# Gathering the RG-LRU gate products of a hybrid decoder layer into four runs on TensorE

## The chip, the cores and the metric

The kernel runs on one core of one Trainium2 chip. The metric is device time in microseconds: the median over runs. Each core has the engines TensorE (PE in the profile), VectorE (DVE), ScalarE (ACT), GpSimd (POOL) and SyncE (SP, which issues most DMAs).

## The reference

One decoder layer on 1024 tokens of width 1024, with 16 meta tokens ahead of them. Cut to what matters here:

```python
u = rmsnorm(h, g_pre_mix)
q, k, v, xr, yr = split(u @ w_in)           # 512, 128, 128, 512, 512 columns
attn = sliding_window_attention_with_sinks(q, k, v, sinks)     # window 128
xr = causal_depthwise_conv(xr, conv_w, conv_b)                 # width 4
# RG-LRU: 8 blocks of 64 channels
r = sigmoid(einsum(xr, w_a) + b_a)          # the gates: a 64x64 product a block
i = sigmoid(einsum(xr, w_x) + b_x)
a = exp(-8 * r * softplus(-lam))
hr = scan(a, sqrt(1 - a*a) * i * xr)        # h[t] = a[t] h[t-1] + u[t]
rec = gelu(yr) * hr
h = h + rmsnorm(concat(attn, rec) @ w_out)
h = h + rmsnorm(relu(rmsnorm(h) @ w_ff1)**2 @ w_ff2)
```

## The kernel before

Every float32 operand of a matmul is split into a rounded high part and a low part (`split`, L94: a cast, mostly on ACT, then a subtraction on DVE), and a product is the sum of three matmuls, high by high, high by low and low by high (`mm3`, L123). Activations lie with channels on the 128 partitions and tokens along the row, in two pieces of 512 columns (`REAL2`) or three of at most 348 (`THIRDS`).

The input projection of a chunk of 128 channels against all tokens is `project` (L265): for each piece a bank of PSUM under the tag `acc` (two buffers), 24 matmuls into it, then a `sink` that copies the bank out. For the y columns there are four chunks, y0 to y3, each 2 x 24 matmuls; their sink is a DVE copy (L752). In the profile these matmuls appear as L125, L130 and L131 with `ps_acc<-a,ws`.

Attention goes in eight steps of two pairs of heads and a quarter of the tokens: `scores` (products, exponentials on ACT) and `attend` (transposes, POOL selects at L684, six value products a half into a bank `o` at L697, then the bank's two halves summed: an ACT copy at L706 and a DVE addition at L707, twice a step). While attention runs, one further projection is put in a step (`next_fill`, with a priority `FILL_LAG` = 1000 steps back); the last two of these eight are y0 and y1. Then come the gates.

`gates(c)` handles channel chunk c of four: it splits the conv's output, and for each third of the tokens it takes two banks (tags `s`, `pt`, `o` in turn, two buffers each) and issues six matmuls of 64 rows (L819). `s` picks the upper or the lower 64 partitions, so two neighbours with `s` = 0 and 1 use the two row halves of the array. That makes 18 products a chunk, 72 in all. ACT empties each bank with a sigmoid (`lut`, L82). `gather(c)` then exchanges halves between the two gates (DVE at L833, L835 and L836, POOL at L834), and `decay`, `recur` and `rec_out` go on to the recurrence; every function on ACT's tables is kept in program order by `lut`. Projections y2 and y3 and the output projection's products follow.

The order of instructions on each engine is found when the program is built, by a list scheduler with priorities (program order, unless deferred) over a simulated timeline; tiles of a tag wait for a free buffer. `behind(name, ins)` adds an ordering edge for that scheduler and no signal on the chip. `split`, `mm3`, `gates` and `project` are helpers, so one line of the profile may stand for many uses.

Of the kernel before, what the change touches and what calls it, by code (L numbers as in the profile page):

```python
# [9 lines left out]
F32 = mybir.dt.float32  # L10
F32R = mybir.dt.float32r
AF = mybir.ActivationFunctionType
ALU = mybir.AluOpType
# [3 lines left out]
P = 128  # L17
D = 1024
KC = D // P
T = 1024  # L20
NMETA = 16
# [3 lines left out]
NLRU = 4  # L25
# [12 lines left out]
def hybrid_layer(  # L38
# [6 lines left out]
    nc = tc.nc  # L45
# [4 lines left out]
    small = ctx.enter_context(tc.tile_pool(name="small", bufs=4))  # L50
# [4 lines left out]
    bufs = {"raw": 2, "ws": 5, "a": 16, "b": 17, "c": 8, "d": 4, "e": 2}  # L55
    uid = [0]

    def slot(tag, shape, dt=F32):
        uid[0] += 1
        return slab.tile(shape, dt, tag=tag, name=f"{tag}{uid[0]}", bufs=bufs[tag])  # L60

    def pair(tag, shape):
        return slot(tag, shape, F32R), slot(tag, shape, F32R)

    def bank(tag, shape=(P, 512)):
        uid[0] += 1
        return ps.tile(list(shape), F32, tag=tag, name=f"ps_{tag}{uid[0]}")

    def f32(ap):
        return ap.bitcast(F32)  # L70
# [10 lines left out]
    def lut(*args, **kwargs):  # L81
        ins = nc.scalar.activation(*args, **kwargs).ins  # L82
        if last_lut[0] is not None:
            tc.add_manual_dep(
                ins, last_lut[0],
                mybir.DependencyInfo(
                    mybir.DependencyClass.NoSync, mybir.DependencyReason.DATA
                ),
                reason="lut",
            )  # L90
        last_lut[0] = ins.name
        return ins

    def split(hi, lo, src, eng=None):  # L94
        if eng is None:
            nc.scalar.copy(hi, src)  # L96
        else:
            eng.tensor_copy(hi, src)
        low = nc.vector.tensor_tensor(lo, src, f32(hi), op=ALU.subtract).ins  # L99
        mark[0] = low.name  # L100
        return low
# [4 lines left out]
    def behind(name, *inss):  # L106
        for ins in inss:
            tc.add_manual_dep(
                ins, name,
                mybir.DependencyInfo(  # L110
                    mybir.DependencyClass.NoSync, mybir.DependencyReason.DATA
                ),
                reason="order",
            )
# [8 lines left out]
    def mm3(dst, lhs, rhs, start, stop, after=None):  # L123
        (lh, ll), (rh, rl) = lhs, rhs
        ins = nc.tensor.matmul(  # L125
            dst, lh, rh, start=start, stop=False, skip_group_check=True
        ).ins
        if after:
            behind(after, ins)
        nc.tensor.matmul(dst, lh, rl, start=False, stop=False, skip_group_check=True)  # L130
        last_mm[0] = nc.tensor.matmul(  # L131
            dst, ll, rh, start=False, stop=stop, skip_group_check=True
        ).ins.name
# [50 lines left out]
    eps_col = const.tile([P, 1], F32, name="eps_col")  # L184
# [44 lines left out]
    u = [pair("a", [P, TT]) for _ in range(KC)]  # L229
# [32 lines left out]
            chained(1, ins)  # L262
        return xn

    def project(w, pieces, sink):  # L265
        wh, wl = w
        for t0, n in pieces:
            acc = bank("acc")
            for kc in range(KC):
                uh, ul = u[kc]  # L270
                mm3(
                    acc[:, :n], (wh[:, kc, :], wl[:, kc, :]),
                    (uh[:, t0 : t0 + n], ul[:, t0 : t0 + n]),
                    kc == 0, kc == KC - 1,
                )
            sink(acc[:, :n], t0, n)

# [11 lines left out]
    REAL2 = [(16, 512), (528, 512)]  # L289
# [209 lines left out]
    for b in range(4):  # L499
# [3 lines left out]
        if b == 0:  # L503

            acc = [bank("acc"), bank("acc")]
# [11 lines left out]
            for w, (t0, n), sink, tag in (  # L517
                (wq, (16, 256), sink_q0, "o"), (wq1, (16, 256), sink_q1, "acc"),
            ):
                acc = bank(tag)  # L520
# [10 lines left out]
    for h in range(2):  # L531
        r, o, m = HALF[h], HALF[1 - h], slice(P - NMETA, 2 * P)
# [77 lines left out]
    def scores(jp, quarter):  # L610
# [57 lines left out]
            )  # L668
        return sn

    def attend(jp, quarter, sn):
        flat = sn.rearrange("p a b c -> p (a b c)")
        pp = []
        for h in range(2):

            ph, pl = (slot("c", [P, 4, 2, P], F32R) for _ in range(2))
            pt = bank("pt")
            for i in range(4):
                nc.tensor.transpose(pt[:, i * P : (i + 1) * P], sn[:, h, i, 0:P], ident)
            pt = pt.rearrange("p (a b) -> p a b", a=4)  # L680
            split(ph[:, :, 0], pl[:, :, 0], pt)
            for p_ in (ph, pl):
                for s, g, op in ((1, 1, ALU.is_ge), (0, -1, ALU.is_gt)):
                    nc.gpsimd.affine_select(  # L684
                        out=p_[:, :, s], in_=f32(p_[:, :, 0]), pattern=[[0, 4], [g, P]],
                        compare_op=op, fill=0.0, base=0, channel_multiplier=-g,
                    )
            pp.append((ph, pl))
        kb0 = 2 * quarter
        for h in range(2):  # L690
            po = bank("o")
            two = po.rearrange("p (j c) -> p j c", j=2)
            for n, (oc, pc, w) in enumerate(((0, 0, P), (0, P, 2 * P), (P, 3 * P, P))):
                kb = kb0 + n
                v = vk[h][:, kb - 1, :] if kb else vm[:, h, :]
                for k, p_ in enumerate(pp[h]):
                    nc.tensor.matmul(  # L697
                        two[:, :, oc : oc + w], v,
                        p_.rearrange("p (j i) s c -> p j (i s c)", j=2)[:, :, pc : pc + w],
                        start=n == 0 and k == 0, stop=n == 2 and k == 1,  # L700
                        skip_group_check=True,
                    )

            r, o = HALF[h], HALF[1 - h]
            whole = flat[r, 0:512]
            nc.scalar.copy(whole, po[o, :])  # L706
            nc.vector.tensor_tensor(whole, po[r, :], whole, op=ALU.add)  # L707
        ah, al = at[quarter // 2][jp]
        c = slice(256 * (quarter % 2), 256 * (quarter % 2) + 256)
        split(  # L710
            ah[:, :, c], al[:, :, c],
            flat[:, 0:512].rearrange("p (j c) -> p j c", j=2),
        )
# [4 lines left out]
    def conv(c, xr, tag="d"):  # L718
# [9 lines left out]
            )  # L728
        xc[c] = y

    ys, y_copies = [None] * NLRU, {}

    def fill_q(j):
# [13 lines left out]
    def fill_y(c):  # L747
        def run(w):
            y = slot("b" if c in (1, 2) else "d", [P, T])

            def sink(acc, t0, n):
                ins = nc.vector.tensor_copy(y[:, t0 - NMETA : t0 - NMETA + n], acc).ins  # L752
                y_copies.setdefault(c, ins.name)

            project(w, REAL2, sink)
            ys[c] = y
        return run

    qs = [q0, q1, None, None]
    fills = []  # L760
# [7 lines left out]
    loaded = [fills[0][0]()]  # L768

    def next_fill():  # L770
        i = len(loaded) - 1
        if i + 1 < len(fills):
            loaded.append(fills[i + 1][0]())
        else:
            loaded.append(None)
        fills[i][1](loaded[i])

    prev = None
    for jp in range(2):
        at_pair(jp)  # L780
        for quarter in range(4):
# [4 lines left out]
            if prev is not None:  # L786
                attend(*prev)
            prev = (jp, quarter, sn)
    attend(*prev)


# [10 lines left out]
    nc.vector.tensor_tensor(gw[:, 1], graw, f32(gw[:, 0]), op=ALU.subtract)  # L802

    rg = [None] * NLRU

    def gates(c):
        ch, cl = pair("b", [P, TT])
        split(ch, cl, xc[c])


        z = [slot("c", [P, TT]) for _ in range(2)]
        for t0, n in THIRDS:
            acc = []
            for s in range(2):
                flip[0] += 1
                acc.append(bank(("s", "pt", "o")[flip[0] % 3]))
            for k, (a, b) in enumerate(((0, ch), (0, cl), (1, ch))):
                for s in range(2):
                    nc.tensor.matmul(  # L819
                        acc[s][:, :n], gw[HALF[s], a, c, :], b[HALF[s], t0 : t0 + n],  # L820
                        start=k == 0, stop=k == 2, skip_group_check=True,
                    )
            for s in range(2):
                lut(
                    z[s][:, t0 : t0 + n], acc[s][:, :n], AF.Sigmoid,
                    bias=prm[:, c, 5 + s : 6 + s],
                )
        rg[c] = z


    def gather(c):
        z, gi = rg[c], slot("b" if c > 1 else "c", [P, TT])
        first = nc.vector.tensor_copy(gi[HALF[0]], z[0][HALF[1]]).ins  # L833
        nc.gpsimd.tensor_copy(z[0][HALF[1]], z[1][HALF[1]])  # L834
        nc.vector.tensor_copy(gi[HALF[1]], z[1][HALF[0]])  # L835
        nc.vector.tensor_tensor(gi, gi, xc[c], op=ALU.mult)  # L836
        rg[c] = z[0], gi
        return first
# [38 lines left out]
        wo[kc] = pair(tag, [P, D])  # L877
        split(wo[kc][0], wo[kc][1], wo_raw[kc], eng)

    for c in range(NLRU):  # L880
        gates(c)
        if c < 2:
            gather(c)
    next_fill()
    for c in (2, 3):
        behind(y_copies[2], gather(c))
    next_fill()
# [275 lines left out]
    for t in range(8):  # L1163
        po = pos[t] if t < 4 else out_banks(t)
# [191 lines left out]
    for n, p in enumerate(third):  # L1356
# [10 lines left out]
        if p not in a12_early:  # L1367
            y2 = bank(("acc", "s")[p % 2])
# [192 lines left out]
```

## Time and profile before

| | |
|---|---|
| median of 3 runs | 949.5 us (949.23 to 949.68) |
| the profiled execution | 949.03 us, span 947.3 us |
| TensorE | 937.9 us busy, 4584 matmuls |
| VectorE | 664.4 us busy |
| ScalarE | 505.0 us busy |
| GpSimd | 135.9 us busy |
| DMA | 134.91 MB, mean 142 GB/s |
| granted TensorE clock | 0.998 |

In the profile's lines, PE is TensorE's matmul, PEld its weight load, and `out<-in` names the written and the read tiles. In a timeline, the columns are the start, the duration, the engine, the line and the tiles; in brackets stands the engine's idle time before the instruction and what ended it. Matmuls are pipelined and their durations overlap, so the distance from start to start is the measure of what one costs.

### The profile page before, as it was taken

What the parts mean: (1) busy time and instruction counts of PE and PEld (TensorE: products, weight loads), DVE (VectorE), ACT (ScalarE), POOL (GpSimd) and SP (SyncE); (2) the same over time, 40 slices, a digit from 0 to 9 for tenths busy, and PEclk for the clock granted to TensorE, in tenths of its full rate; (3) what the DMA queues carried; (4) which work ended last, traced back from release to release, by engine and by line L of the source; (5) the groups of instructions that cost most, each with busy time, mean ns of one, the idle gap of its engine ahead of it and who ended that gap; (6) DMA issues with size and microseconds to landing.
All of it is one profiled execution on the core that took longest, in us unless ns stands there. A gap on an engine that the chain in (4) does not pass through costs nothing.

```text
span 947.3 us, 12174 instructions
## 1 busy us (share of the span) xinstructions
PE 937.9 (99%) x4584; PEld 784.8 (83%) x4584; DVE 664.4 (70%) x849; ACT 505.0 (53%) x844; POOL 135.9 (14%) x205
## 2 busy tenths in 40 slices
PE   9999999999999999999999999999999999999996
PEld 8999999878888878888888888888888888888885
DVE  6667788779977987665544465476667676779783
ACT  8546765569634664443655575654533443445441
POOL 4104437431021100010000000001111000001201
PEclk9999999999999999999999999999999999999999
DMA  8220011104259658574422363334777655537934
GB/s 273 57 68 23 24 45 45 45 23 141 82 194 273 200 180 283 188 258 134 156 89 89 111 215 120 109 111 114 198 170 178 206 179 192 194 126 209 238 64 89
DMA packets 97366, 134.91 MB, mean 142 GB/s; under 512 B 22230, under 2 KB 61158, under 8 KB 97308
## 3 DMA queue, kind: packets, MB, share of 16 engines
q1 hardware_dynamic: 87996, 108.64, 35.3%
q0 software_dynamic: 8880, 24.19, 11.9%
q10 hardware_dynamic: 432, 1.31, 0.4%
q8 instruction: 36, 0.59, 0.3%
q14 instruction: 22, 0.18, 0.1%
HBM read 112.55 MB, written 20.97 MB: 141 GB/s over the span
## 4 chain that ended last, share of the span: by engine, by line
PE 97%; DVE 1%; DMA 0%; ACT 0%; issue 0%; SPq 0%; DVEq 0%
PE ps_acc L125 12%; PE ps_acc L131 12%; PE ps_acc L130 12%; PE ps_pt L131 6%; PE ps_s L131 6%; PE ps_pt L125 6%; PE ps_pt L130 6%; PE ps_s L125 6%; PE ps_s L130 6%; PE ps_o L125 5%; PE ps_o L131 5%; PE ps_o L130 5%; PE ps_o L697 2%; PE ps_acc L282 1%; PE ps_s L629 1%; PE ps_s L633 1%
## 5 line engine op out<-in xcount | busy, mean ns | idle before, releaser
L99 DVE TENSOR_TENSOR ws<-raw,ws 128x1024 fp32r<-128x1024 f32 (+1 forms) x69 | 82.3, 1193 | 72.4 <-PE ps_o L130 23.1
L96 ACT CAST ws<-raw 128x1024 fp32r<-128x1024 f32 (+1 forms) x68 | 69.8, 1027 | 82.0 <-PE ps_o L130 33.6
L96 ACT CAST ws<-e 128x1024 fp32r<-128x1024 f32 x41 | 43.0, 1050 | 85.8 <-PE ps_o L130 38.2
L130 PE MATMUL ps_acc<-a,ws 128*128 128x512 f32 (+3 forms) x240 | 82.9, 346 | 0.0
L125 PE MATMUL ps_acc<-a,ws 128*128 128x512 f32 (+3 forms) x240 | 82.8, 346 | 0.0
L131 PE MATMUL ps_acc<-a,ws 128*128 128x512 f32 (+3 forms) x240 | 82.2, 343 | 0.0
L99 DVE TENSOR_TENSOR b<-b,b 128x1024 fp32r<-128x1024 f32 (+2 forms) x50 | 59.0, 1179 | 27.9 <-PE ps_o L130 22.6
L99 DVE TENSOR_TENSOR ws<-e,ws 128x1024 fp32r<-128x1024 f32 x41 | 50.2, 1223 | 31.7 <-ACT ws L96 18.4
L96 ACT CAST b<-b 128x1024 fp32r<-128x1024 f32 (+2 forms) x49 | 50.0, 1020 | 41.8 <-DVE b L1029 35.5
L684 POOL TENSOR_SCALAR_AFFINE_SELECT c<-c 128x512 fp32r<-128x512 f32 x64 | 55.0, 873 | 73.7 <-ACT c L96 64.2
L125 PEld LDWEIGHTS ps_acc<-a,ws 128*128 128x128 f32 x240 | 45.2, 189 | 4.3 <-issue 0.7
L131 PEld LDWEIGHTS ps_acc<-a,ws 128*128 128x128 f32 x240 | 45.2, 188 | 3.7 <-issue 0.2
L130 PEld LDWEIGHTS ps_acc<-a,ws 128*128 128x128 f32 x240 | 45.2, 188 | 3.6 <-issue 0.4
L131 PE MATMUL ps_acc<-ws,b 128*128 128x512 f32 (+1 forms) x120 | 46.3, 386 | 0.0
L130 PE MATMUL ps_acc<-ws,b 128*128 128x512 f32 (+1 forms) x120 | 46.2, 385 | 0.0
L125 PE MATMUL ps_acc<-ws,b 128*128 128x512 f32 (+1 forms) x120 | 46.0, 385 | 0.0
L125 PE MATMUL ps_pt<-ws,b 128*128 128x512 f32 x112 | 44.3, 395 | 0.0
L131 PE MATMUL ps_pt<-ws,b 128*128 128x512 f32 x112 | 44.2, 395 | 0.0
L130 PE MATMUL ps_pt<-ws,b 128*128 128x512 f32 x112 | 44.1, 394 | 0.0
L131 PE MATMUL ps_s<-ws,b 128*128 128x512 f32 x110 | 43.4, 394 | 0.0
L130 PE MATMUL ps_s<-ws,b 128*128 128x512 f32 x110 | 43.4, 394 | 0.0
L125 PE MATMUL ps_s<-ws,b 128*128 128x512 f32 x110 | 43.3, 394 | 0.0
(417 smaller groups left out, 2660.0 us busy)
## 6 DMA issues: line engine op xcount, KB each, us to landing
raw<-in_w_ff_dram SPq DMA_DIRECT2D x59, 512.0 KB, 3.9
e<-in_w_ff_dram SPq DMA_DIRECT2D x43, 512.0 KB, 3.5
a<-in_w_ff_dram SPq DMA_DIRECT2D x12, 512.0 KB, 6.0
s_dram<-a POOLq DMA_DIRECT2D x12, 512.0 KB, 4.1
raw<-in_w_in_dram SPq DMA_DIRECT2D x9, 512.0 KB, 3.6
c<-in_x_dram SPq DMA_DIRECT2D x8, 512.0 KB, 4.5
d<-in_x_dram SPq DMA_DIRECT2D x8, 512.0 KB, 3.4
out_dram<-raw SPq DMA_DIRECT2D x8, 512.0 KB
```

The lines of the kernel that those rows point to most:

```text
L96: nc.scalar.copy(hi, src)
L99: low = nc.vector.tensor_tensor(lo, src, f32(hi), op=ALU.subtract).ins
L125: ins = nc.tensor.matmul(dst, lh, rh, start=start, stop=False, skip_group_check=True).ins
L130: nc.tensor.matmul(dst, lh, rl, start=False, stop=False, skip_group_check=True)
L131: last_mm[0] = nc.tensor.matmul(dst, ll, rh, start=False, stop=stop, skip_group_check=True).ins.name
L282: last_mm[0] = nc.tensor.matmul(acc[:, :n], w[k // 2][:, kc, :], u[kc][k % 2][:, t0 : t0 + n], start=k == 0 and kc == 0, stop=k == last an ...
L629: nc.tensor.matmul(dst, q[h][:, c], hi, start=True, stop=False, skip_group_check=True,)
L633: nc.tensor.matmul(dst, q[h][:, c], lo, start=False, stop=True, skip_group_check=True,)
L684: nc.gpsimd.affine_select(out=p_[:, :, s], in_=f32(p_[:, :, 0]), pattern=[[0, 4], [g, P]], compare_op=op, fill=0.0, base=0, channel_multip ...
L697: nc.tensor.matmul(two[:, :, oc : oc + w], v, p_.rearrange("p (j i) s c -> p j (i s c)", j=2)[:, :, pc : pc + w], start=n == 0 and k == 0, ...
```

## The change

The gate products of a chunk are chained one behind the other, so that each chunk's 18 products stand together on PE. The first chunk's run is ordered behind the last DVE addition that reads a bank of value products (`drained`). y2 is no longer projected by `next_fill` but by `y2_products`: its first 24 products after the first chunk's gates in program order, not held; then five behind gates(0) and ahead of gates(1), five between gates(1) and gates(2), five between gates(2) and gates(3), and the last nine behind gates(3). y3's projection is held behind the last gate product, and its weights are loaded ahead of the gates. A sigmoid of one column stands in ACT's table order ahead of the first gate sigmoid.

```diff
--- before.py
+++ after.py
@@ -262,7 +262,7 @@
             chained(1, ins)
         return xn
 
-    def project(w, pieces, sink):
+    def project(w, pieces, sink, after=None):
         wh, wl = w
         for t0, n in pieces:
             acc = bank("acc")
@@ -271,7 +271,7 @@
                 mm3(
                     acc[:, :n], (wh[:, kc, :], wl[:, kc, :]),
                     (uh[:, t0 : t0 + n], ul[:, t0 : t0 + n]),
-                    kc == 0, kc == KC - 1,
+                    kc == 0, kc == KC - 1, after if kc == 0 else None,
                 )
             sink(acc[:, :n], t0, n)
 
@@ -668,6 +668,8 @@
             )
         return sn
 
+    drained = [None]
+
     def attend(jp, quarter, sn):
         flat = sn.rearrange("p a b c -> p (a b c)")
         pp = []
@@ -704,7 +706,9 @@
             r, o = HALF[h], HALF[1 - h]
             whole = flat[r, 0:512]
             nc.scalar.copy(whole, po[o, :])
-            nc.vector.tensor_tensor(whole, po[r, :], whole, op=ALU.add)
+            drained[0] = nc.vector.tensor_tensor(
+                whole, po[r, :], whole, op=ALU.add
+            ).ins.name
         ah, al = at[quarter // 2][jp]
         c = slice(256 * (quarter % 2), 256 * (quarter % 2) + 256)
         split(
@@ -728,6 +732,7 @@
             )
         xc[c] = y
 
+    gate_end = [None]
     ys, y_copies = [None] * NLRU, {}
 
     def fill_q(j):
@@ -752,7 +757,7 @@
                 ins = nc.vector.tensor_copy(y[:, t0 - NMETA : t0 - NMETA + n], acc).ins
                 y_copies.setdefault(c, ins.name)
 
-            project(w, REAL2, sink)
+            project(w, REAL2, sink, gate_end[0])
             ys[c] = y
         return run
 
@@ -802,10 +807,13 @@
     nc.vector.tensor_tensor(gw[:, 1], graw, f32(gw[:, 0]), op=ALU.subtract)
 
     rg = [None] * NLRU
+    warm = small.tile([P, 1], F32, name="warm", tag="warm", bufs=1)
+    lut(warm, eps_col, AF.Sigmoid)
 
     def gates(c):
         ch, cl = pair("b", [P, TT])
         split(ch, cl, xc[c])
+        start = last_mm3[0] if c else drained[0]
 
 
         z = [slot("c", [P, TT]) for _ in range(2)]
@@ -816,16 +824,22 @@
                 acc.append(bank(("s", "pt", "o")[flip[0] % 3]))
             for k, (a, b) in enumerate(((0, ch), (0, cl), (1, ch))):
                 for s in range(2):
-                    nc.tensor.matmul(
+                    ins = nc.tensor.matmul(
                         acc[s][:, :n], gw[HALF[s], a, c, :], b[HALF[s], t0 : t0 + n],
                         start=k == 0, stop=k == 2, skip_group_check=True,
-                    )
+                    ).ins
+                    if start:
+                        behind(start, ins)
+                    start = ins.name
+            gate_end[0] = start
             for s in range(2):
                 lut(
                     z[s][:, t0 : t0 + n], acc[s][:, :n], AF.Sigmoid,
                     bias=prm[:, c, 5 + s : 6 + s],
                 )
         rg[c] = z
+
+    last_mm3 = [None]
 
 
     def gather(c):
@@ -877,11 +891,45 @@
         wo[kc] = pair(tag, [P, D])
         split(wo[kc][0], wo[kc][1], wo_raw[kc], eng)
 
-    for c in range(NLRU):
+    loaded.append(fills[9][0]())
+    y2 = slot("b", [P, T])
+    wh, wl = loaded[8]
+    done_mm = 0
+
+    def y2_products(count):
+        nonlocal done_mm
+        for m in range(done_mm, done_mm + count):
+            half, kc, k = m // 24, m % 24 // 3, m % 3
+            t0, n = REAL2[half]
+            if m % 24 == 0:
+                y2_bank.append(bank("acc"))
+            uh, ul = u[kc]
+            ins = nc.tensor.matmul(
+                y2_bank[half], (wh, wh, wl)[k][:, kc, :],
+                (uh, ul, uh)[k][:, t0 : t0 + n],
+                start=m % 24 == 0, stop=m % 24 == 23, skip_group_check=True,
+            ).ins
+            if m == done_mm and m >= 24:
+                behind(gate_end[0], ins)
+            last_mm3[0] = ins.name
+            if m % 24 == 23:
+                copied = nc.vector.tensor_copy(
+                    y2[:, t0 - NMETA : t0 - NMETA + n], y2_bank[half]
+                ).ins
+                y_copies.setdefault(2, copied.name)
+        done_mm += count
+
+    y2_bank = []
+    gates(0)
+    gather(0)
+    y2_products(24)
+    for c in range(1, NLRU):
+        y2_products(5)
         gates(c)
         if c < 2:
             gather(c)
-    next_fill()
+    y2_products(48 - done_mm)
+    ys[2] = y2
     for c in (2, 3):
         behind(y_copies[2], gather(c))
     next_fill()
```

## The prediction

> **What bounds the kernel now.** I read the page first, then the PE groups and PE's timeline where the gate products stand, then the timelines of ACT, DVE and POOL over the same stretch, and last the place where PE next waits. The page:
>
> ```profile
> span 947.3 us, 12174 instructions
> ...
> PE 97%; DVE 1%; DMA 0%; ACT 0%; issue 0%; SPq 0%; DVEq 0%
> ```
>
> The chain that ended last is TensorE work nearly everywhere, so an edit is worth what it takes off PE's stream, less what PE then has to wait. The gate products lie among the y products. The groups of PE between two y products, the starts at 193.17 and 213.08 us:
>
> ```profile
> L819 PE MATMUL ps_s<-b,e 64*128 64x348 f32 x24 | 5.6, 341 | 0.0
> L819 PE MATMUL ps_pt<-b,e 64*128 64x348 f32 (+1 forms) x24 | 5.6, 349 | 0.0
> L130 PE MATMUL ps_acc<-a,ws 128*128 128x512 f32 x13 | 5.3, 410 | 0.0
> L819 PE MATMUL ps_o<-b,e 64*128 64x348 f32 (+1 forms) x24 | 5.2, 335 | 0.0
> L125 PE MATMUL ps_acc<-a,ws 128*128 128x512 f32 x12 | 5.1, 429 | 0.0
> L131 PE MATMUL ps_acc<-a,ws 128*128 128x512 f32 x13 | 5.1, 393 | 0.0
> L697 PE MATMUL ps_o<-c,b 128*128 128x256 f32 (+1 forms) x6 | 1.5, 354 | 0.0
> ```
>
> So this stretch of 213.08 - 193.17 = 19.91 us holds all 72 gate products (3 x 24), six value products (L697), and 12 + 13 + 13 y products with the last one's start as its end, that is 37 whole y intervals. Busy times overlap here, so I go by starts. PE's timeline (start, duration):
>
> ```profile
> 190.50 0.97 PE L697 MATMUL ps_o<-c,b 128*128 128x256 f32 x5
> 191.31 0.40 PE L130 MATMUL ps_acc<-a,ws 128*128 128x512 f32 x1
> ...
> 193.17 0.39 PE L125 MATMUL ps_acc<-a,ws 128*128 128x512 f32 x1
> ...
> 206.38 0.39 PE L131 MATMUL ps_acc<-a,ws 128*128 128x512 f32 x1
> 206.70 0.43 PE L819 MATMUL ps_pt<-b,e 64*128 64x348 f32 x1
> ...
> 206.97 0.32 PE L819 MATMUL ps_pt<-b,e 64*128 64x348 f32 x1
> ...
> 208.08 0.32 PE L819 MATMUL ps_s<-b,e 64*128 64x348 f32 x1
> ...
> 208.33 0.50 PE L125 MATMUL ps_acc<-a,ws 128*128 128x512 f32 x1
> 208.67 0.40 PE L130 MATMUL ps_acc<-a,ws 128*128 128x512 f32 x1
> ...
> 213.08 0.50 PE L131 MATMUL ps_acc<-a,ws 128*128 128x512 f32 x1
> ...
> 224.23 0.40 PE L131 MATMUL ps_acc<-a,ws 128*128 128x512 f32 x1
> ```
>
> The run from 206.70 to 208.08 is one of nine pairs, each pair on the two row halves side by side. It gives the prices. From the second pair to the ninth: (208.08 - 206.97) / 7 = 0.159 us a pair. From 213.08 to 224.23 lie 48 y intervals, the first behind a run; (11.15 - 0.11) / 48 = 0.230 us a y product. Around the run, four steps are longer than these: 206.38 to 206.70 is 0.32 (0.09 over), the first pair takes 0.27 (0.11 over), the last pair 0.25 (0.09 over), and 208.33 to 208.67 is 0.34 (0.11 over). Going into the half-height products and out again costs 0.40 us a run.
>
> **What the 72 products cost now, and in four runs.** Five value products take 191.31 - 190.50 = 0.81 us; the sixth I estimate at a fifth of that, 0.16. The stretch less its other work is 19.91 - 37 x 0.230 - 0.97 = 10.43 us for the gates. In four whole runs they cost 4 x (9 x 0.159 + 0.40) = 7.32 us. **PE's stream loses 3.1 us.** The rest of the 10.43 is crossings, and products that ran with no partner.
>
> **The hold and the one-column sigmoid.** ACT and POOL, with the idle time before and what ended it in brackets:
>
> ```profile
> 196.01 1.28 ACT L82 ACT_TABLE_LOAD   x1 [3.86 <-PE ps_s L819]
> 197.31 0.55 ACT L82 ACTIVATE c<-ps_s,prm 128x348 f32<-128x348 f32 x1
> 197.88 0.58 ACT L706 COPY c<-ps_o 64x512 f32<-64x512 f32 x1
> 198.48 1.06 ACT L96 CAST b<-b 128x1040 fp32r<-128x1040 f32 x1
> ...
> 199.89 0.61 ACT L96 CAST b<-c 128x512 fp32r<-128x512 f32 x1
> 200.40 0.55 ACT L82 ACTIVATE c<-ps_o,prm 128x348 f32<-128x348 f32 x1
> 200.85 0.55 ACT L82 ACTIVATE c<-ps_s,prm 128x348 f32<-128x348 f32 x1
> ...
> 214.02 0.56 ACT L82 ACTIVATE c<-ps_o,prm 128x344 f32<-128x344 f32 x1
> ```
>
> ```profile
> 189.29 4.82 POOL L684 TENSOR_SCALAR_AFFINE_SELECT c<-c 128x512 fp32r<-128x512 f32 x3 [0.36 <-DVE c L99]
> ```
>
> Today the first gate sigmoid and its table load stand on ACT ahead of the copy at L706, and that copy's DVE partner (L707) is the read behind which the change holds the first gate product. With the gates held, ACT has nothing ahead of L706. POOL's selects end at 189.29 + 4.82 = 194.1; the five value products end some 0.9 us later; L706 (0.58) and L707 (0.69) with hand-overs bring the read's end to about 197.0. On PE meanwhile: of y2's first 24 products 14 are left at 193.17 (38 to the end of both halves, less 24), so without gates they reach 193.17 + 14 x 0.230 + 0.97 = 197.4. The hold therefore leaves no hole, with 0.4 us to spare; each microsecond of later read beyond that costs PE one. Behind the held product on PE nothing else is queued that could run but these y products. The warm-up sigmoid itself lies in ACT's 3.86 us of idle time; by size it lies between nothing and the 0.55 of a 348-column one, I take under 0.3, and the 1.28 load only moves.
>
> The Trainium skill (ScalarE: Activation LUTs, What ACT_TABLE_LOAD costs) gives a set switch as 1283 ns and a drain of 1380 ns besides. Here the load's 1.28 agrees, but the sigmoid starts 1.30 after the load did, so no drain is seen behind it. By the page's 2.66 the warm-up still fits the 3.86, and the sum stays.
>
> **The wait that comes in.** The second half of y2 needs an acc bank that y1's second half holds until its copy (L752) has run on DVE. The waits name it, and DVE's timeline shows why that copy is late:
>
> ```profile
> PEld ps_acc L125 <- DVE b L752: 0.2, 1, 0.2
> ```
>
> ```profile
> 198.49 0.69 DVE L707 TENSOR_TENSOR c<-ps_o,c 64x512 f32<-64x512 f32 x1 [4.29 <-ACT c L706]
> 200.53 0.69 DVE L99 TENSOR_TENSOR b<-c,b 128x512 fp32r<-128x512 f32 x1 [1.35 <-ACT b L96]
> 201.14 1.22 DVE L99 TENSOR_TENSOR ws<-raw,ws 128x1024 fp32r<-128x1024 f32 x1
> 202.28 0.69 DVE L98 CAST ws<-raw 128x1024 fp32r<-128x1024 f32 x1
> 202.98 0.69 DVE L752 COPY b<-ps_acc 128x512 f32<-128x512 f32 x1
> ...
> 211.80 0.70 DVE L833 COPY b<-c 64x1040 f32<-64x1040 f32 x1
> ...
> 215.15 1.21 DVE L99 TENSOR_TENSOR ws<-raw,ws 128x1024 fp32r<-128x1024 f32 x1
> ```
>
> The copy ends at 203.67. Today PE filled that time with gate products of any chunk. Afterwards the five y products stand ahead of gates(1), all of which waits behind them, and PE has nothing else. PE gets there when the first 24 and gates(0) are done: 197.4 + 1.83 = 199.2. In today's order the copy's end follows L707's start by 203.67 - 198.49 = 5.18 us, of which 1.35 is idle time for a cast on ACT that stood behind a sigmoid and another cast; without these about 0.55 of it is left, so 4.4 us, and the copy ends at 196.3 + 4.4 = 200.7: a hole of 1.5 us. The other end: the split of y3's weights (201.14, 1.14 to the next start) is now emitted ahead of the gates and can run in the gap before L707, so the copy ends at 199.6 and the hole is 0.4. I take 1.0. Later y products find their banks copied.
>
> y3's load moves up in program order with its DMA; that had long been issued:
>
> ```profile
> 161.28 0.37 SPq L208 DMA_DIRECT2D raw<-in_w_in_dram  x1
> ```
>
> It passes nothing on SP that is still waiting in this stretch, so nothing for it, and nothing on POOL's queue moves.
>
> **Banks of the later runs.** Each run fills six banks, and its thirds wait for the sigmoids of the run before. A sigmoid comes every 0.45 (200.40 to 200.85), six take 2.7; PE's cycle is 1.83 + 5 x 0.230 = 2.98. PE stays the longer one by 0.28 a cycle. The casts of 1.06 and 0.61 fall once each, so a wait of at most 0.5 in one run; I take 0.
>
> **Next in line.** The products of the output projection wait a little for DVE already:
>
> ```profile
> 258.60 0.39 PE L130 MATMUL ps_pt<-a,b 128*128 128x512 f32 x1
> 259.02 0.50 PE L131 MATMUL ps_pt<-a,b 128*128 128x512 f32 x1
> ```
>
> A step of 0.42 against 0.23, and one of 0.34 behind it: no slack for a gain on PE alone. But this DVE work follows the gates through ACT. The last sigmoid, at 214.02 now, would come at about 200.2 (199.2 and the hole) + 3 x 2.98 + 1.0 = 210.1, four microseconds earlier, and DVE's idle 4.29 shrinks too. The gathers of chunks 2 and 3 stay behind y2's first copy, which comes earlier; their sigmoids come later than it in any case. So DVE keeps up, and up to 0.3 of wait goes: I take 0.3.
>
> **Sum.** -3.1 + 1.0 - 0.3 = -2.4 us. The profiled execution took 949.03 (span 947.3 and 1.7 around it), 0.5 under the median of 949.5; against the median the forecast is **947.1**. What a measurement can tell from no change is 0.2%, 1.9 us. Its own range: the hole from 0 to 1.6 and the wait at 258.6 give -3.4 to -1.5, so 946.1 to 948.0.
>
> **The rivals.**
> 1. *The bank's copy queues behind chunk 0's gather, slower.* y1's products and copies carry a priority 1000 steps back, so DVE takes it only when nothing else is ready. Gates(0) end at 199.2 at the latest, their sigmoids 1.7 us or so later with a cast between, about 200.9; a gather takes 3.35 (211.80 to 215.15) and the copy 0.69: 204.9. PE's hole is 5.7, the net +2.6, 952.1. It turns to a loss once the copy ends after 199.2 + 3.1 = 202.3; at today's 203.67 it is already +1.4. Against it: the copy is ready before 191, and DVE has gaps until 200.
> 2. *The gain ends at 258.6.* If DVE's chain doesn't move, PE arrives 2 to 3 us early and waits: 949.3. For it: PE is level with DVE there. Against: the sigmoids lead that chain and move.
> 3. *Evictions bound the runs.* The Trainium skill (TensorEngine Tiling (Array Packing), PSUM Bottleneck) says that tiling speeds up the products and not the copying out. As a mechanism of this kernel: with both casts put between the sigmoids, and y copies late on DVE, each of three runs waits 0.5, and 1.5 is given back: 948.6. The rows have it 2.7 against 2.98, so narrowly not.
> 4. *The hold does little.* It orders instructions when the program is built, and no signal on the chip belongs to it. If gates still stand alone or in pieces, 949.5.
>
> **How the numbers follow.** Forecast 0.57, rival 1 0.16, rival 2 0.10, rival 3 0.10, rival 4 0.07. Faster: the forecast but for 0.06 of it where the hole is full, and 0.05 of rival 3: 0.56. Slower: rival 1 and 0.01 of mishaps from rival 3: 0.17. The rest, 0.27, lies within. Range: from the whole gain with no hole and a little more after it, 945.8, to 951.0, which leaves out the worse part of rival 1.
>
> **What would show it.** Right: L819 in four runs of nine pairs, 0.159 apart, with one step of 0.4 to 1.5 us ahead of the first y product behind gates(0), ended by L752; the table load well ahead of L706; the last sigmoid near 210; y3's last product near 222. Wrong: a step of over 3 us there, waits for L82 inside the later runs, or at 258 a longer wait for DVE than now.

## The result, and the profile after

The changed kernel takes 953.1 us (median of nine executions, 950.5 to 953.7) against 949.7 us (949.2 to 951.0) for the kernel before, run beside it on the same chip. The ratio is 1.0025, with a 95% interval of 1.0016 to 1.0034: slower by a quarter of a per cent, where 947.1 was forecast. The nine executions lie in two groups, five from 953.1 to 953.7 us with a mean granted clock of 0.996 and four from 950.5 to 951.6 with 0.997 to 0.998; the profiled one, 953.5 us, is of the first, and so is the median, whose quotient of 1.0036 overstates the ratio (the means give 1.0026).

From the page of the changed kernel (span 951.8 us), the engines of the chain that ended last:

```profile
PE 89%; DVE 3%; ACT 2%; DMA 2%; issue 1%; SPq 1%; DVEq 0%; ACTq 0%
```

TensorE's share of that chain fell from 97% to 89%; DVE, ACT and DMA now have 7% between them. To find the place I numbered PE's 4584 matmuls, as many as before, and compared the starts of matmuls of the same number. The offset (after less before) is +1.8 us at 30 us, still +1.8 at 190, -0.2 from 217 to 254, +4.0 at 264 and +4.1 at 925. The first 1.8 us arise ahead of 30 us, in code that the change doesn't touch, where a transfer of x landed later; the profiles of the other kernels have 0.0 to 1.5 there. That leaves two events: **the gate products gave 2.0 us, and 257 to 265 us took 4.2.** Their net, 2.2 us, is close to the 2.4 us of the ratio.

PE's timeline of the gate products (start, duration, instruction, idle time and what ended it; x2 or x5 stands for a row of alike matmuls):

```profile
199.23 0.43 PE L827 MATMUL ps_s<-b,e 64*128 64x348 f32 x1
...
201.16 1.42 PE L907 MATMUL ps_acc<-a,ws 128*128 128x512 f32 x5
202.51 0.42 PE L827 MATMUL ps_s<-b,e 64*128 64x348 f32 x1
...
203.42 0.32 PE L827 MATMUL ps_s<-b,e 64*128 64x348 f32 x1
203.92 0.42 PE L827 MATMUL ps_pt<-b,e 64*128 64x344 f32 x1 [0.19 <-ACT c L82]
204.36 0.42 PE L827 MATMUL ps_o<-b,e 64*128 64x344 f32 x1
...
205.02 1.42 PE L907 MATMUL ps_acc<-a,ws 128*128 128x512 f32 x5
206.37 0.42 PE L827 MATMUL ps_s<-b,e 64*128 64x348 f32 x1
...
208.00 1.41 PE L907 MATMUL ps_acc<-a,ws 128*128 128x512 f32 x5
209.34 0.43 PE L827 MATMUL ps_s<-b,e 64*128 64x348 f32 x1
...
210.97 1.88 PE L907 MATMUL ps_acc<-a,ws 128*128 128x512 f32 x7
```

The four runs are there, with five y products between them. The first five stand directly behind the first run, with no hole. Instead two steps inside the second run, 203.42 to 203.92 and on to 204.36, are 0.50 and 0.44 where a pair needs 0.16. ACT shows why:

```profile
183.59 1.28 ACT L82 ACT_TABLE_LOAD   x1
184.88 0.20 ACT L82 ACTIVATE warm<-eps_col 128x1 f32<-128x1 f32 x1
...
202.35 1.07 ACT L96 CAST b<-b 128x1040 fp32r<-128x1040 f32 x1
203.30 0.57 ACT L82 ACTIVATE c<-ps_pt,prm 128x344 f32<-128x344 f32 x1
203.74 0.57 ACT L82 ACTIVATE c<-ps_o,prm 128x344 f32<-128x344 f32 x1
...
212.36 0.57 ACT L82 ACTIVATE c<-ps_o,prm 128x344 f32<-128x344 f32 x1
```

The table load and the one-column sigmoid (0.20 us) stand well ahead of the gates. The cast at 202.35 stands between the first run's sigmoids, so the banks of its last third come free late. The last sigmoid starts at 212.36, or 210.6 less the 1.8 us from the beginning.

Then the loss. PE's timeline:

```profile
257.93 0.50 PE L125 MATMUL ps_pt<-a,b 128*128 128x512 f32 x1 [0.26 <-ACT b L96]
...
259.68 0.50 PE L131 MATMUL ps_pt<-a,b 128*128 128x512 f32 x1 [1.03 <-DVE b L99]
...
261.49 0.79 PE L131 MATMUL ps_pt<-a,b 128*128 128x512 f32 x1 [0.84 <-DVE b L99]
...
262.50 0.63 PE L130 MATMUL ps_pt<-a,b 128*128 128x512 f32 x1
262.93 0.63 PE L131 MATMUL ps_pt<-a,b 128*128 128x512 f32 x1
```

And the busy time of each engine in two stretches, with the granted clock behind it (PEclk):

```profile
core 0: us, PE busy (x) PEld busy (x) DVE busy (x) ACT busy (x) POOL busy (x), PEclk, DMA share, GB/s
257.00:261.00 4.00, 2.36 (x8) 0.97 (x7) 4.00 (x8) 3.22 (x6) 0.00 (x0) 1.00 0.00 0
261.00:265.00 4.00, 3.51 (x8) 2.82 (x9) 1.64 (x3) 0.81 (x3) 0.00 (x0) 0.57 0.72 231
```

These are the output products that need the second pair's `rec_out`. Before, the one wait here was 0.2 us; now PE stands idle three times, ended by DVE's low parts (L99) and ACT's cast (L96). Directly behind, the granted clock falls to 0.57 in the mean, and products start 0.43 us apart instead of 0.23. Of 4.5 us that the steps from 257.27 to 265.01 have over 0.23 each, 2.8 are the waits with the step behind each, and 1.7 the slower products (one of 0.59, six of 0.43, one of 0.37); the wait of before had 0.3.

Why DVE was late stands 20 us earlier. ACT before, and ACT after:

```profile
222.81 1.03 ACT L96 CAST a<-raw 128x1024 fp32r<-128x1024 f32 x1
...
231.05 1.05 ACT L96 CAST a<-raw 128x1024 fp32r<-128x1024 f32 x1
233.43 0.62 ACT L96 CAST b<-d 128x512 fp32r<-128x512 f32 x1 [1.33 <-DVE d L858]
234.07 1.28 ACT L82 ACT_TABLE_LOAD   x1
235.36 1.17 ACT L82 ACTIVATE b<-c,m8sp 128x1040 f32<-128x1040 f32 x1
```

```profile
228.45 1.05 ACT L96 CAST a<-d 128x1024 fp32r<-128x1024 f32 x1
231.31 1.05 ACT L96 CAST a<-raw 128x1024 fp32r<-128x1024 f32 x1 [1.81 <-DMA raw<-in_w_out_dram]
236.09 1.05 ACT L96 CAST a<-d 128x1024 fp32r<-128x1024 f32 x1 [3.73 <-DMA d<-in_w_out_dram]
237.04 0.61 ACT L96 CAST b<-d 128x512 fp32r<-128x512 f32 x1
238.02 1.05 ACT L96 CAST a<-raw 128x1024 fp32r<-128x1024 f32 x1 [0.36 <-DMA raw<-in_w_out_dram]
239.09 1.28 ACT L82 ACT_TABLE_LOAD   x1
240.38 1.17 ACT L82 ACTIVATE b<-c,m8sp 128x1040 f32<-128x1040 f32 x1
```

The 128 x 1040 activation from `m8sp` is `decay(2)`. Before, five casts of `w_out`'s row tiles (222.81 to 231.05 us) and the first pair's `rec_out` cast stand ahead of it, and none of the five waits for its transfer. After, two more weight casts do, those of row tiles 6 and 7, and the last three of the seven wait for their transfers: 1.81 + 3.73 + 0.36 = 5.9 us of idle ACT. The raw tiles have two buffers under each of two tags, which come free when DVE has made the low parts: the three transfers are issued at 227.94, 231.29 and 234.64 us, just where three of DVE's low parts end. DVE after, and below it the line of DVE before that answers to its last:

```profile
227.82 2.32 DVE L867 TENSOR_TENSOR_SCAN c<-b,c 128x1040 f32<-128x1040 f32 x1
...
231.18 2.32 DVE L867 TENSOR_TENSOR_SCAN c<-b,c 128x1040 f32<-128x1040 f32 x1
...
236.26 1.29 DVE L872 TENSOR_TENSOR d<-d,c 128x512 f32<-128x512 f32 x2
...
247.49 2.39 DVE L865 SCALAR_TENSOR_TENSOR c<-b,c 128x1040 f32<-128x1040 f32 x2 [3.79 <-ACT c L82]
```

```profile
243.28 1.24 DVE L851 SCALAR_TENSOR_TENSOR c<-b,c 128x1040 f32<-128x1040 f32 x1 [0.38 <-ACT c L82]
```

Both scans and the weights' low parts stand ahead of `rec_out`'s product (L872; L858 before, where it started at 232.71, between the scans). The second pair's `recur` starts at 247.49 (before, L851 at 243.28) after 3.79 us of waiting for ACT's square root.

### The profile page after: what moved, and what is told of

Read it like the earlier page. It is cut to its first block, busy times and chain, and to the rows that moved or that the text cites. A ratio compares the mean times of both kernels' runs of the same rounds, so it can differ in the third digit from the quotient of the medians.

```text
span 951.8 us, 12179 instructions
## 1 busy us (share of the span) xinstructions
PE 938.7 (99%) x4584; PEld 784.3 (82%) x4584; DVE 664.5 (70%) x849; ACT 504.8 (53%) x845; POOL 134.6 (14%) x205
## 4 chain that ended last, share of the span: by engine, by line
PE 89%; DVE 3%; ACT 2%; DMA 2%; issue 1%; SPq 1%; DVEq 0%; ACTq 0%
PE ps_acc L131 10%; PE ps_acc L125 10%; PE ps_acc L130 10%; PE ps_pt L131 6%; PE ps_s L131 6%; PE ps_pt L125 6%; PE ps_pt L130 6%; PE ps_s L125 6%; PE ps_s L130 6%; PE ps_o L125 5%; PE ps_o L130 5%; PE ps_o L131 5%; PE ps_o L699 2%; ACT c L82 1%; DMA c<-in_x_dram 1%
## 5 line engine op out<-in xcount | busy, mean ns | idle before, releaser
L99 DVE TENSOR_TENSOR ws<-raw,ws 128x1024 fp32r<-128x1024 f32 (+1 forms) x69 | 82.3, 1193 | 69.7 <-PE ps_o L130 22.9
L96 ACT CAST ws<-raw 128x1024 fp32r<-128x1024 f32 (+1 forms) x68 | 69.7, 1026 | 82.7 <-PE ps_o L130 33.3
L96 ACT CAST ws<-e 128x1024 fp32r<-128x1024 f32 x41 | 43.0, 1049 | 85.1 <-PE ps_o L130 37.7
L99 DVE TENSOR_TENSOR b<-b,b 128x1024 fp32r<-128x1024 f32 (+2 forms) x50 | 58.9, 1178 | 27.3 <-PE ps_o L130 22.1
L130 PE MATMUL ps_acc<-a,ws 128*128 128x512 f32 (+3 forms) x224 | 76.3, 341 | 0.0
L125 PE MATMUL ps_acc<-a,ws 128*128 128x512 f32 (+3 forms) x224 | 76.2, 340 | 0.0
L131 PE MATMUL ps_acc<-a,ws 128*128 128x512 f32 (+3 forms) x224 | 75.8, 338 | 0.0
L99 DVE TENSOR_TENSOR ws<-e,ws 128x1024 fp32r<-128x1024 f32 x41 | 50.1, 1223 | 31.2 <-ACT ws L96 17.7
L96 ACT CAST b<-b 128x1024 fp32r<-128x1024 f32 (+2 forms) x49 | 50.0, 1020 | 40.8 <-DVE b L1077 35.3
L131 PEld LDWEIGHTS ps_acc<-a,ws 128*128 128x128 f32 x224 | 42.1, 188 | 3.0
L125 PEld LDWEIGHTS ps_acc<-a,ws 128*128 128x128 f32 x224 | 42.2, 188 | 2.9
L130 PEld LDWEIGHTS ps_acc<-a,ws 128*128 128x128 f32 x224 | 42.1, 188 | 2.9
```

The source lines that it names most:

```text
L125: ins = nc.tensor.matmul(dst, lh, rh, start=start, stop=False, skip_group_check=True).ins
L131: last_mm[0] = nc.tensor.matmul(dst, ll, rh, start=False, stop=stop, skip_group_check=True).ins.name
```

## The experiments

Every ratio is against the kernel before, run beside it on the same chip, with its 95% interval; medians of 6 to 11 executions.

**Is the tail's order the cause?** First the changed kernel with the second pair's decays emitted ahead of the first pair's `rec_out`, and so ahead of the later weight casts.

```diff
         for c in cs:
-            decay(c)
+            if av[c] is None:
+                decay(c)
...
+        if cs[0] == 0:
+            decay(2)
+            decay(3)
         at[0][2 + cs[0] // 2] = pair("b", [P, 2, 512])
```

> The changed kernel, with the decays of chunks 2 and 3 issued in program order ahead of the first pair's output step, so that ScalarE takes them some 10 us earlier and the weight casts come later. Theory (order of ScalarE): no wait for the recurrence at 258 us; 946.5 to 949, if TensorE doesn't now wait for weights 2 to 5. Rival (VectorE bound): VectorE's chain ends as late as in the changed kernel, 951 to 953. Third: the wait moves to the weights, near 235 us, 949 to 952.

Measured: 947.7 us, ratio 0.9982 (0.9974 to 0.9991), faster than the kernel before and the changed one. ACT of this kernel:

```profile
225.50 1.17 ACT L82 ACTIVATE b<-c,m8sp 128x1040 f32<-128x1040 f32 x1
```

`decay(2)` starts at 225.50 instead of 240.38, so its inputs had been there long before ACT came to it in the changed kernel: 14.9 us by the two traces, of which 1.5 lies in their first 30 us. PE has no wait from 254 to 262 us, and the clock there is 1.00. One wait is left, PE's timeline:

```profile
226.84 0.40 PE L125 MATMUL ps_s<-ws,b 128*128 128x512 f32 x1
227.65 0.73 PE L125 MATMUL ps_pt<-a,b 128*128 128x512 f32 x2 [0.41 <-ACT a L96]
```

The other way round: the kernel before, with none of the change, but with the loads and casts of `w_out`'s row tiles 6 and 7 put ahead of the second decays.

```diff
-        lut(av[c], r, AF.Exp, scale=m8sp[:, c : c + 1])
+        exp = lut(av[c], r, AF.Exp, scale=m8sp[:, c : c + 1])
+        if cast[0] and c > 1:
+            behind(cast[0], exp)
...
-        for kc in range(4 + cs[0], 6 + cs[0]):
-            load_wo(kc, ("d", "raw")[kc % 2])
-            split_wo(kc, "a")
+        if cs[0] == 0:
+            for kc in range(4, 8):
+                load_wo(kc, ("d", "raw")[kc % 2])
+                split_wo(kc, "a")
```

> The kernel before, with nothing of the change, but with the casts of output-projection weights 6 and 7 put ahead of the second pair's decays on ScalarE, as the changed kernel has them. Theory (order of ScalarE): the order alone makes the wait at 258 us, without any gain at the gates: 952 to 955 us. Rival (the gates' order delays VectorE itself): 949.5, as before.

Measured: 951.7 us, ratio 1.0024 (1.0016 to 1.0033), a little under the theory's range. Its `decay(2)` starts at 241.14, PE waits at 257.8, 259.0 and 261.7 (steps of 0.91, 1.43 and 0.52), and the offset to before rises by 2.2 us there. So this order alone makes the waits and a loss of 2.2 us, without any change in the gate products. It does not make all of the 4.2 us: the clock stays at 1.00 here, and the slower products are missing.

The one-column sigmoid alone, on the kernel before:

```diff
+    warm = small.tile([P, 1], F32, name="warm", tag="warm", bufs=1)
+    lut(warm, eps_col, AF.Sigmoid)
```

> The kernel before with the one-column sigmoid alone. Theory: the table load leaves the place ahead of the last value copy, TensorE's order hardly changes and ScalarE's later order stays: 948.8 to 949.7. Rival (the sigmoid is what turns ScalarE's later order): 951 or more.

Measured: 949.6 us, ratio 1.0003 (0.9994 to 1.0011). It costs and brings nothing that can be measured, and the tail keeps its order.

Then the changed kernel with only the casts of row tiles 6 and 7 ordered behind the last decay on ACT.

```diff
-        lut(r, r, AF.Tanh, scale=m4sp[:, c : c + 1])
+        decay_end[0] = lut(r, r, AF.Tanh, scale=m4sp[:, c : c + 1]).name
...
-            split_wo(kc, "a")
+            split_wo(kc, "a", None, decay_end[0] if kc > 5 else None)
```

> The changed kernel, with the casts of output-projection weights 6 and 7 ordered behind the second pair's decays on ScalarE; nothing else. Theory (order of ScalarE): TensorE's gain of 2.0 us at the gates is real, and it is lost at 257 to 265 us because those casts, waiting for their DMAs, hold up the second table load (239.09 us). Then the wait there falls under 1.5 us, the granted clock stays at 1.0, and the kernel takes 947.0 to 949.5 us. Rival (VectorE bound): VectorE's own work is late whatever ScalarE's order; then the wait of some 4 us stays and the time is that of the changed kernel, 951 to 953.

Measured: 955.8 us, ratio 1.0063 (1.0051 to 1.0075): worse, and outside both forecasts. ACT then waits 4.76 us for DVE's `rec_out` product, and the table load for the decays starts at 236.38, so they gain little. The two casts alone were not the block: the `rec_out` cast ahead of the decays waits on DVE as well, behind two scans and the low parts. And the low parts of the two delayed casts (1.2 us each, at 245.94 and 252.75) now stand on DVE inside the second pair's chain, so at 258 us 5.5 us are lost. A second step of 2.6 us comes at 340 us, where PE waits for a cast of another tile (ACT, L96), again with slower products behind it; what moved that cast I did not follow.

Last, which part of the change turns the order. The changed kernel without the hold, its tail untouched:

```diff
-        start = last_mm3[0] if c else drained[0]
+        start = last_mm3[0] if c else None
```

> The changed kernel (953.1 us) without the hold on the first run and nothing else, its tail untouched. Theory A (the tail's order on ScalarE flips because the gate products end earlier and in runs, whether held or not): the second pair's decays still stand behind w_out's casts, TensorE waits for VectorE at 257 to 262 us by 1 us or more, 951.0 to 953.5, with or without the halved clock behind it. Theory B (the hold is what moves the tail's order): the decays start within 1 us of the kernel before (235.4 us), no wait at 258 us over 0.4 us, 947.5 to 949.5.

Measured: 949.5 us, ratio 1.0002 (0.9993 to 1.0011). The time and the decays are those of theory B, but the wait at 258 us is not. ACT and PE of this kernel:

```profile
232.68 1.05 ACT L96 CAST a<-raw 128x1024 fp32r<-128x1024 f32 x1 [3.21 <-DMA raw<-in_w_out_dram]
...
235.89 1.17 ACT L82 ACTIVATE b<-c,m8sp 128x1040 f32<-128x1040 f32 x1
237.38 1.05 ACT L96 CAST a<-d 128x1024 fp32r<-128x1024 f32 x1 [0.32 <-DMA d<-in_w_out_dram]
```

```profile
257.80 0.40 PE L130 MATMUL ps_pt<-a,b 128*128 128x512 f32 x1
259.04 0.50 PE L131 MATMUL ps_pt<-a,b 128*128 128x512 f32 x1 [0.84 <-DVE b L99]
```

The decays are back near 235.4, with five weight casts ahead of them as before. But the first of these stands behind the first pair's gelus, at 225.59 as in the changed kernel (before, 222.81), the fifth waits 3.21 us for its transfer, and the sixth stands between the decays and waits too. The gate products give 1.3 us, and 0.9 of it is lost again at 257.8. So the hold is what puts the casts of tiles 6 and 7 ahead of the decays; the rest of the change moves the first casts back. By which comparison of the build it does so I did not follow.

**Does the halved clock follow TensorE's idle time?** The changed kernel with four products of zeros, added to an output bank ahead of the waiting products:

```diff
+    nc.gpsimd.memset(vmt, 0.0)
...
+        if t == 0:
+            for i in range(NFILL):
+                ins = nc.tensor.matmul(
+                    po[0], vmt, f32(wo[5][0][:, 0:512]), start=False,
+                    stop=False, skip_group_check=True,
+                ).ins
```

> The changed kernel (953.1 us) with four full-width products of zeros added to an output bank ahead of the two products groups that wait at 258 us; they add nothing to the sum. They keep TensorE busy for some microseconds of the 257 to 262 us in which it waits there. Theory A (the granted clock of 0.50 to 0.53 from 262 to 265 us follows TensorE's waits just ahead): the clock stays near 1.0, the twelve products at 0.427 us become 0.23, and the time is 950.5 to 951.7. Theory B (the lower clock has another cause, or the filler only moves the wait): 952.7 to 954 or more, with products at 0.427 us after it.

Measured: 951.1 us, ratio 1.0022 (1.0013 to 1.0030). The median is 2.0 us below the changed kernel's. PE, and the two stretches again:

```profile
256.30 3.60 PE L1217 MATMUL ps_pt<-a,vmt 128*128 128x512 f32 x8
259.33 0.79 PE L125 MATMUL ps_pt<-a,b 128*128 128x512 f32 x1
259.96 0.40 PE L130 MATMUL ps_pt<-a,b 128*128 128x512 f32 x1
```

```profile
257.00:261.00 4.00, 4.00 (x13) 2.19 (x12) 4.00 (x8) 2.29 (x5) 0.00 (x0) 1.00 0.23 72
261.00:265.00 4.00, 4.00 (x19) 3.25 (x18) 1.28 (x4) 2.06 (x6) 0.56 (x1) 1.00 0.58 193
```

VectorE is as late as in the changed kernel (the second pair's `recur` starts at 246.30, 1.2 us earlier, as all of this execution does), yet the clock stays at 1.00 and no step at 0.43 follows the zeros. The eight rows of zeros, two to a product, take 3.0 us and the step behind them is 0.63, a little more than the 2.8 us of waiting that they fill; without the slower products the offset of the rest rises by 3.2 us instead of 4.2. That is theory A for the clock. In the times it is not shown: the medians are 2.0 us apart, but the intervals of the two ratios, 1.0022 and 1.0025, overlap nearly in full.

**What are the gate products worth, and the hold?** The rest stands on the 947.7 us kernel. The casts of `w_out`'s second to fourth row tiles ahead of the second decays on ACT, against the wait at 226.84:

```diff
+        exp = lut(av[c], r, AF.Exp, scale=m8sp[:, c : c + 1])
+        if c > 1:
+            behind(cast[0], exp)
```

> The same kernel (decays ahead) with the casts of the second to fourth row tiles of w_out ordered ahead of the second pair's decays on ScalarE; in the 947.7 us kernel the first output products wait 0.81 us at 226.84 us for such a cast. Theory A (that wait is the cast's place alone): it goes, 946.8 to 947.2. Theory B (VectorE then takes the low parts of these tiles ahead of its read of the first pair's gated result, and the wait at 258 us comes back): 948.5 to 951. If the output products at 258 us do not wait and the 0.81 us stays, a transfer and not the cast is late: 947.5 to 947.9.

Measured: 947.4 us, ratio 0.9980 (0.9971 to 0.9988), a little over theory A's range. The wait is gone and none returns at 258: offset +0.3 ahead of the gates, -1.7 behind them, -1.9 at 264, -2.3 at 925. Nearly the same tail on the kernel before, with nothing of the change:

> The kernel before (949.2 us) with the tail of the best one (second pair's decays ahead of the first pair's gated result, the casts of w_out's second to fourth row tiles ahead of them) and nothing of the change in the gate products. Theory A (the gain of the 947.4 us kernel over the one before comes from the gate products' four runs, and the tail's order is worth only the 0.3 us wait at 258.6 us): 948.7 to 949.2. Theory B (the order of the tail is what gains, the runs of gate products nothing): 947.2 to 947.8. Theory C (the gate products' old end holds the decays and this order makes the output products wait): over 949.6.

Measured: 949.9 us, ratio 1.0006 (0.9997 to 1.0015); offset 0.0 to 250 us, +0.3 at 264. The tail by itself gains nothing. The time lies in theory C's range, but the trace shows 0.3 us of its waits. Between the two kernels lie (1.0006 - 0.9980) x 949.3 = 2.5 us, and the intervals do not overlap. That is not the change alone, since the tails differ in one place: this edit puts the second decays ahead of the first pair's gelus on ACT (the gelus start at 235.53), the one above behind them (222.09). In the traces 2.0 of the difference arises at the gates and 0.5 from there to 264 us. The 2.0 stands on firmer ground: each of the five kernels with the hold and five y products gains it at the gates, whatever its tail.

Eight y products instead of five between the runs, without that order of the casts:

```diff
-        y2_products(5)
+        y2_products(8)
```

> The same kernel with eight y products instead of five between the runs, so that all 24 products of y2's second half lie between the four runs and each later run begins 0.7 us later after the one ahead of it. Theory A (what is left in the gate products is two waits for a bank that sigmoids free, 0.505 - 0.23 and 0.437 - 0.23 inside the second run and as much at the first): the waits go, the last matmul moves 0.5 to 0.9 us earlier, 946.8 to 947.2. Theory B (the steps over 0.3 us are crossings of tile and not waits): 947.5 to 947.9. Theory C (later gates make the last sigmoid and so the decays later, and the tail pays): over 948.2.

Measured: 947.4 us, ratio 0.9983 (0.9974 to 0.9991), between the ranges of theories A and B. At the gates it gives 2.6 us instead of 2.0: both long steps inside the second run are gone, so they were waits for the bank. But a wait of 0.8 us comes at 230.2, for a weight's cast. Both steps together:

> Both steps together on the kernel with the decays ahead: eight y products between the runs, and the casts of w_out's second to fourth row tiles ahead of the second pair's decays. Eight alone moved the matmuls behind the gate products 2.65 us earlier than before instead of 2.03, and then lost 0.98 us at 230.2 us to a weight's cast (947.44); the cast order alone took away the wait of 0.81 us (947.38). Theory A (the two are separate costs): offset of -2.6 us to the kernel before from the gates to the end, 946.4 to 946.9. Theory B (the output products are held from 228 us by the decays' own end and not by the casts' order, so later gates give back what they win): 947.2 to 947.6.

Measured: 947.2 us, ratio 0.9975 (0.9965 to 0.9985), the lowest ratio, but not told apart from 0.9980. Of 2.7 us at the gates, 0.2 is lost by 229 us, 0.5 at 233 and 0.4 at 257 (steps of 0.57 and 0.78). The time is theory B's: the output products are level with DVE again, and later gates give back what they win.

The same two kernels without the hold, first without and then with the order of the casts:

> The kernel with the second pair's decays ahead (947.7 us) without the hold: the first run may start at the first sigmoid instead of behind the last value bank's read. Theory A (the hold is worth something because it keeps the first run in one piece): the first run is cut into pieces that wait for sigmoids, each 0.2 to 0.9 us, and the time is 948.3 to 949.0. Theory B (the gate products are paced by the sigmoids whatever stands ahead; the hold does nothing): 947.4 to 948.0. Theory C (the hold delays the sigmoids' start and costs time): 946.7 to 947.3.

> The kernel with decays ahead and the casts ahead of them (947.38 us), without the hold on the first run. Without the hold, but without that order of the casts, the matmuls behind the gate products stood 1.35 us earlier than just ahead of them, against 2.03 to 2.05 with it, and 2.0 us went to waits for weights at 228 to 231 us. Theory A (those waits were the casts' order and the hold itself is worth the 0.7 us): 947.9 to 948.3. Theory B (without the hold the gates end later and the waits stay): 949.0 to 949.8. Theory C (the hold is worth nothing): 947.2 to 947.6.

Measured: 949.6 us (1.0004, 0.9995 to 1.0013), above all three forecasts, and 947.3 us (0.9978, 0.9968 to 0.9987), theory C's range. In both traces the gates give 1.3 to 1.4 us instead of 2.0, since single pairs again cross in and out between y and value products; the first loses 1.9 us more to waits for weights at 228 to 232. The 0.7 us of the hold is seen in the traces, but not in the times of the second.

## Why the prediction was wrong

- **The gate term came out right by luck.** Forecast: -3.1 for the runs and +1.0 for a hole, -2.1 together; the trace has -2.0. But three misses cancel: the hole was 0, waits for banks that stood at 0 took 0.6, and the runs themselves are worth some 2.6, what the kernel with eight y products gains at the gates without hole or bank waits.
- **The hole was not there, and another cost took its place.** Forecast was y2's second half waiting for the copy at L752. But y2's first half went ahead of y1's second (its copy, L916, starts at 195.81), so that bank was free. The term was 0. What I had put at 0, "Banks of the later runs", came instead: steps of 0.50 and 0.44 for a pair's 0.16, about 0.6 together, and some at the ends of the first two runs. Rival 3 named this mechanism and the casts on ACT, for three runs; it came in full only in the second, and eight y products took it away.
- **The failed step is "Next in line": "So DVE keeps up", with 0.3 us to gain.** Instead 4.2 us were lost there. I reasoned from the sigmoids (forecast 210.1, measured 210.6 after the late start: right) straight to the products at 258 us. Between them lie `decay`, `recur` and `rec_out` on two engines whose order is found anew at each build. The sigmoids ended 3.4 us earlier and the decays began 5.0 us later (3.2 without the late start). The prediction works from no row of ACT or DVE between 216 and 258 us.
- **Rival 2 named the place**, but its worst case was a chain that doesn't move: no gain, 949.3. It moved back, and the price was 4.2 us. Without the hold the time came near that rival's, 949.5, though there too the chain had moved back, by 1.75 us at `recur` (245.03 against 243.28).
- **The halved clock was in no term.** I priced a wait as its length alone; here 2.8 us of waiting brought 1.7 us of slower products with it.

## What to carry to other kernels

Where an order is found by the build, an edit can reorder work tens of microseconds behind it: follow the chain back from the next place where the bounding engine waits, row by row, to the edit, and name every instruction that could change places. Before judging such an edit, pin the order behind it, and put the order that it brought on the kernel without it; here the first turned 1.0025 into 0.9980, and the second, at 1.0024, showed that the order and not the edit costs the time. See that two kernels that are to differ in one thing do so: the two tails above did not. And several waits of TensorE close together can cost more than their length.

## What the runs showed of the hardware

The granted clock fell to one half behind waits that were not long, for 3.41 us in the changed kernel (from 261.52) and for 6.83 and 3.41 us in the kernel with the later casts (from 259.11 and 344.44), by the clock records of the traces. These times are one and two of a grid: in each of the fourteen traces the times between two changes of the clock are whole multiples of 3.413 us (682.67 is 200 of them, 78.51 is 23). So the stretch to look at is the one of the grid that ends where the clock falls. In the changed kernel, in the kernel with the later casts (its second fall, at 344.44, has 1.69 us there), and in the kernel before with the turned order, whose clock did not fall:

```profile
258.11:261.52 3.41, 1.54 (x6) 0.63 (x6) 3.41 (x7) 2.37 (x5) 0.00 (x0) 1.00 0.13 23
```

```profile
255.70:259.11 3.41, 1.70 (x7) 0.81 (x5) 3.41 (x5) 1.09 (x3) 0.00 (x0) 1.00 0.00 0
```

```profile
258.54:261.95 3.41, 2.23 (x8) 1.35 (x8) 3.41 (x7) 2.69 (x6) 0.00 (x0) 1.00 0.00 0
```

In all fourteen traces, the ends of the programs with them, the clock, where it was full, fell after every stretch of the grid in which TensorE was busy for 1.70 us or less, and after none with 1.96 or more: here half of a stretch idle is enough. The longest step from one product to the next was 1.42 us ahead of the fall in the changed kernel and 2.58 ahead of the one at 344.44, so several short waits do as well as one. What decides is also where the grid lies: by it the same waits can fall into one stretch or two. One stretch at one half takes 0.5 x 3.41 / 951 = 0.0018 off the mean clock, an estimate from these figures, and that is the distance of 0.996 from 0.998 in the result; the other executions have no trace that could show it.

The Trainium skill (TensorE: Matmul & The Clock Gate, What's actually happening) has the clock halved after an idle window of about 3.4 us, and the window running freely. The traces agree with a window of 3.41 us, but it need not be idle throughout. At that section's 1.2 GHz a product of 512 columns would take 0.427 us, an estimate; the steps measured were 0.42 to 0.43.
